# A seven-product stage on one Trainium2 core: the sixth product's weights move to another ring of buffers, and two ordinary steps stand between two pairs

## The chip, the cores and the metric

The kernel runs on one core of a Trainium2 chip. Its engines are TensorE (PE in the rows, its weight loads PEld), VectorE (DVE), ScalarE (ACT), GpSimd (POOL) and SyncE (SP, which here only issues transfers). The metric is the device time of one execution in microseconds (us); lower is better.

## The reference

Two layers of a sequence model over 256 positions of width 2048 are computed in float32, and a final norm. The change lies in the second one (the "odd" layer), whose input projection is cut here to what matters:

```
h = rms_norm(x, norm)                    # 256 x 2048
z = h @ w_in                             # 2048 x 6160, split into:
q, k, v, a_lr, gc, u, vd, gd = split(z)  # 512, 512, 1024, 16, 1024, 1024, 1024, 1024 columns
o  = gla_chunked(q, k, v, log_sigmoid(a_lr @ w_alpha + b_alpha) / 16)
yc = rms_norm(o, head_norm) * silu(gc)
yd = spatial_gating(gelu(u), gelu(vd), w_s, b_s, v_norm) * silu(gd)
x  = x + concat(yc, yd) @ w_out
```

## The kernel before, in words

**Weights.** A product with weights is done in 512 KB pieces of 128x1024. SP issues the load of a piece into a buffer of one of three rings: `raw` (3 buffers), `rx` (4) and `ry` (4). `parts` then splits the piece: ScalarE writes a rounded high half (`whi`, L138), VectorE subtracts it for the low half (`wlo`, L73), and TensorE takes three matmuls for each 512 columns and 128 rows of tokens: high weights, low weights, high weights again with the low half of the tokens. There are 4 buffers each of `whi` and `wlo`. A buffer of a ring may be loaded again once ScalarE and VectorE have read it. Outside the pairs the pieces take the rings in turn.

**Ordinary steps.** An ordinary step is one piece with both halves of the tokens, 12 matmuls (lines L146 to L148). The columns gc and gd are done this way, 32 steps in a `Stream`; while the pairs run, their pieces go through `raw` alone.

**Pairs.** The columns q and k, the two halves of vd, and the two halves of u are done as three pairs, each by `pair`. A pair takes two blocks of 512 columns as a two by two block product in seven products instead of eight. A product is four steps, a step is one piece with one form of the tokens, 6 matmuls (lines L251 to L253). In code order the products are: 

- `m12` with four pieces `x0`, loaded ahead. Behind each step GpSimd adds another 512 KB of weights onto the same buffer in flight (an accumulating transfer, L245 in the profile).
- `m3` with four pieces `y0`, and again an addition onto each of them.
- a first product into `m56` with the changed `x0`, and a second addition onto each.
- `m7` with the changed `y0`.
- a second product into the same `m56` with `x0`, now changed twice. Below this is "the last product before the tail".
- the tail: a further product into `m12` with four new pieces `z0`, and `m4` with `x0`, onto which VectorE has added `z0` (L299). The two are interleaved piece by piece, and four VectorE operations on the finished sums (L279 to L283) stand ahead of `m4`.

So a pair has 28 steps, 12 additions in flight, and 24 pieces of transfer. `weave` puts ordinary steps between its steps: 10, 8 and 10 in the three pairs; the last 4 of the 32 follow behind the third. Behind a pair its sums are used: by five or six scaled products on VectorE behind the first (`eb`, `enb`, `ebl`), by Gelu, means and variances and a normalisation (`bn_stats`, `bn_aggr`, and twelve operations in `normed`) behind the second, by Gelu behind the third. Small attention products (`gla`) run beside the second pair, and `mix` beside the end of the third. A scheduler of the framework writes each engine's queue when the program is built; each engine then works through its queue in order.

**Before the change**, `z0` is loaded into `raw`, the ring that the ordinary steps use as well. `x0` of the next pair is loaded during the tail into the ring of this pair's `y0`. So the first and third pair have `x0` in `rx` and `y0` in `ry`, the second pair the other way round.

## Time and profile before

| | |
|---|---|
| median of 3 runs | 898.17 us (897.04 to 899.81) |
| the profiled execution | 898.22 us, its span 896.5 us |
| TensorE | busy 867.7 us of the span, 97%; granted clock 0.987 of full |
| VectorE | busy 610.3 us, 68% |
| ScalarE | busy 525.9 us, 59% |
| transfers | 175.5 MB; SP's queue takes 50.6% of the 16 DMA engines' span, GpSimd's 12.1% |

Busy time is counted from an instruction's start to its end; matmuls overlap, so the distance between two starts is the better measure of TensorE's pace. The times in the rows are microseconds from the start of the span. The first pair's last product before its tail ends near 583 us, the second's near 673 us, the third's near 752 us.

### The profile page before, as it was taken

The page shows a single profiled execution, that of the slowest core. Times are in us where ns is not written, and L with a number is a line of the kernel's source. Part 1 is how long each engine was busy: PE and PEld are TensorE (multiplying, and loading weights), DVE is VectorE, ACT ScalarE, POOL GpSimd, SP SyncE. Part 2 cuts the span into 40 slices and gives each one's busy share as a digit, 9 for nine tenths or more (in the row PEclk, how much of TensorE's full clock was granted, in tenths as well). Part 3 has the DMA queues.
Part 4 walks back from the last instruction along what each step waited for, and adds up shares of the span by engine and source line. Part 5 has one row for each costly group of instructions (what it writes and reads, how often), then busy time and mean ns, then how long its engine had stood idle before and what let it go on. Part 6 is the DMA issues. An engine that isn't in the chain of part 4 may idle for free.

```text
span 896.5 us, 11877 instructions
## 1 busy us (share of the span) xinstructions
PE 867.7 (97%) x4408; PEld 724.3 (81%) x4408; DVE 610.3 (68%) x867; ACT 525.9 (59%) x764; POOL 42.4 (5%) x60
## 2 busy tenths in 40 slices
PE   9999999999999999999999999989997998899996
PEld 7888888888888888888888988866675776688886
DVE  7686556586586577665555987688566885795652
ACT  6755546766756856554445766645574764564532
POOL 0100000000000000000000002101200120000000
PEclk9999999999999999999999999999998999899998
DMA  9896555455364365665535579949953997575502
GB/s 341 337 359 208 196 178 166 151 199 166 130 213 160 110 217 179 194 206 189 186 105 188 192 217 212 293 151 243 217 165 108 254 242 254 194 231 189 187 9 94
DMA packets 50266, 175.53 MB, mean 196 GB/s; under 512 B 5648, under 2 KB 6160, under 8 KB 49952
## 3 DMA queue, kind: packets, MB, share of 16 engines
q1 hardware_dynamic: 43920, 152.65, 50.6%
q0 software_dynamic: 6144, 22.06, 12.1%
q8 instruction: 34, 0.56, 0.3%
q14 instruction: 24, 0.20, 0.1%
q10 hardware_dynamic: 144, 0.07, 0.0%
HBM read 172.66 MB, written 2.10 MB: 195 GB/s over the span
## 4 chain that ended last, share of the span: by engine, by line
PE 82%; DMA 8%; DVE 4%; issue 2%; ACT 2%; POOL 0%; ACTq 0%; POOLq 0%; DVEq 0%; SPq 0%
PE pc L315 20%; PE ps L146 13%; PE ps L148 13%; PE ps L147 13%; PE pc L314 10%; DMA raw<-in_w_in 6%; DVE wlo L73 2%; PE ps L251 2%; PE ps L252 2%; PE ps L253 2%; ACT whi L138 2%; DMA rx<-in_w_in 1%; DVE rx L299 1%; PE pc L317 1%; PE sc L500 1%
## 5 line engine op out<-in xcount | busy, mean ns | idle before, releaser
L315 PE MATMUL pc<-act,whi 128*128 128x512 f32 x768 | 269.7, 395 | 0.0
L314 PE MATMUL pc<-act,wlo 128*128 128x256 f32 x720 | 208.7, 290 | 0.0
L73 DVE TENSOR_TENSOR wlo<-rx,whi 128x1024 fp32r<-128x1024 f32 (+2 forms) x118 | 141.6, 1202 | 77.0 <-ACT whi L138 76.1
L138 ACT CAST whi<-rx 128x1024 fp32r<-128x1024 f32 (+1 forms) x115 | 119.8, 1043 | 90.0 <-PE ps L148 40.3
L73 DVE TENSOR_TENSOR wlo<-ry,whi 128x1024 fp32r<-128x1024 f32 (+2 forms) x110 | 131.7, 1199 | 58.7 <-ACT whi L138 57.5
L315 PEld LDWEIGHTS pc<-act,whi 128*128 128x128 f32 x768 | 142.8, 188 | 29.3
L73 DVE TENSOR_TENSOR wlo<-raw,whi 128x1024 fp32r<-128x1024 f32 (+2 forms) x100 | 119.1, 1191 | 67.8 <-ACT whi L138 67.4
L138 ACT CAST whi<-raw 128x1024 fp32r<-128x1024 f32 (+1 forms) x97 | 100.6, 1038 | 103.8 <-PE ps L148 46.6
L138 ACT CAST whi<-ry 128x1024 fp32r<-128x1024 f32 (+1 forms) x108 | 112.1, 1040 | 77.6 <-PE ps L148 36.6
L146 PE MATMUL ps<-whi,act 128*128 128x512 f32 (+2 forms) x352 | 133.5, 384 | 7.3 <-ACT whi L138 6.9
L314 PEld LDWEIGHTS pc<-act,wlo 128*128 128x128 f32 x720 | 135.9, 189 | 2.4 <-DVE wlo L73 0.8
L147 PE MATMUL ps<-wlo,act 128*128 128x512 f32 (+2 forms) x352 | 133.7, 380 | 0.8 <-DVE wlo L73 0.8
L148 PE MATMUL ps<-whi,act 128*128 128x512 f32 (+2 forms) x352 | 133.3, 379 | 0.0
L146 PE MATMUL ps<-whi,yt 128*128 128x512 f32 (+1 forms) x256 | 97.4, 380 | 0.0
L148 PE MATMUL ps<-whi,yt 128*128 128x512 f32 (+1 forms) x256 | 96.5, 377 | 0.0
L147 PE MATMUL ps<-wlo,yt 128*128 128x512 f32 (+1 forms) x256 | 96.3, 376 | 0.0
L146 PEld LDWEIGHTS ps<-whi,act 128*128 128x128 f32 x352 | 67.1, 192 | 22.2 <-ACT whi L138 8.8
L147 PEld LDWEIGHTS ps<-wlo,act 128*128 128x128 f32 x352 | 67.7, 192 | 14.0 <-DVE wlo L73 2.3
L148 PEld LDWEIGHTS ps<-whi,act 128*128 128x128 f32 x352 | 67.7, 192 | 11.9 <-issue 0.3
L148 PEld LDWEIGHTS ps<-whi,yt 128*128 128x128 f32 x256 | 48.2, 188 | 8.8
L147 PEld LDWEIGHTS ps<-wlo,yt 128*128 128x128 f32 x256 | 48.3, 189 | 8.4
L146 PEld LDWEIGHTS ps<-whi,yt 128*128 128x128 f32 x256 | 48.2, 188 | 8.4
(289 smaller groups left out, 1046.2 us busy)
## 6 DMA issues: line engine op xcount, KB each, us to landing
raw<-in_w_in SPq DMA_DIRECT2D x77, 512.0 KB, 4.8
ry<-in_w_in SPq DMA_DIRECT2D x64, 512.0 KB, 4.9
rx<-in_w_in SPq DMA_DIRECT2D x63, 512.0 KB, 4.6
rx<-in_w_out SPq DMA_DIRECT2D x24, 512.0 KB, 4.6
ry<-in_w_out SPq DMA_DIRECT2D x23, 512.0 KB, 4.6
rx<-in_w_in POOLq DMA_DIRECT2D x20, 512.0 KB, 9.6
raw<-in_w_out SPq DMA_DIRECT2D x17, 512.0 KB, 4.6
ry<-in_w_in POOLq DMA_DIRECT2D x16, 512.0 KB, 9.1
```

The lines of the kernel that those rows point to most:

```text
L73: nc.vector.tensor_tensor(out=o, in0=a, in1=hi.bitcast(F32), op=ALU.subtract)
L138: nc.scalar.copy(hi, raw)
L146: nc.tensor.matmul(ps[b], xh, wh, start=first, stop=False)
L147: nc.tensor.matmul(ps[b], xh, wl, start=False, stop=False)
L148: nc.tensor.matmul(ps[b], xl, wh, start=False, stop=last)
L251: nc.tensor.matmul(ps, xh, wh, start=(first and j == 0), stop=False, skip_group_check=not first)
L252: nc.tensor.matmul(ps, xh, wl, start=False, stop=False, skip_group_check=not first)
L253: nc.tensor.matmul(ps, xl, wh, start=False, stop=(j == 7), skip_group_check=not first)
L299: tc.keep_in_program_order(nc.vector.tensor_tensor(out=x0[i - 1], in0=z0[i - 1], in1=x0[i - 1], op=ALU.add))
L314: nc.tensor.matmul(ps[c][:, 1, :], wl, act[:, k, 0:T], start=False, stop=False)
L315: nc.tensor.matmul(ps[c], wh, act[:, k, :], start=(k == 0), stop=(k == KT - 1))
L317: nc.tensor.matmul(ps[c][:, 1, :], wl, act[:, k, 0:T], start=False, stop=False)
```

## The change

`z0` is loaded into the ring of `y0` (now always `ry`), and this is written earlier in the code, beside the steps of the last product before the tail. The next pair's `x0` is loaded into the ring of this pair's own `x0` (now always `rx`), written behind the `m4` step that uses the buffer last, where it was written behind the `m12` step before. The first and third pair get 8 ordinary steps instead of 10, and two ordinary steps stand behind the first and behind the second pair. Matmuls, splits, additions and transfers are the same in number.

```diff
--- before.py
+++ after.py
@@ -227,7 +227,7 @@
                 stream.step()
                 done += 1
 
-    def pair(w, ua, ub, act, forms, x0, tag, after=None):
+    def pair(w, ua, ub, act, forms, x0, after=None, own="rx", tag="ry"):
 
 
 
@@ -274,7 +274,12 @@
         s5 = mid_tile([P, 512], "s5")
         nc.scalar.copy(s5, m56)
         yield from run(m7, f7, y0, True)
-        yield from run(m56, f6, x0, False)
+
+        z0 = []
+        for i, raw in enumerate(x0):
+            z0.append(fetch(w, ua + 2, i, tag))
+            step(m56, f6, i, raw, False)
+            yield
         t = mid_tile([P, 512], "t")
         nc.vector.tensor_tensor(out=t, in0=m56, in1=s1, op=ALU.subtract)
         c22 = s1
@@ -283,16 +288,14 @@
         nc.vector.tensor_tensor(out=s5, in0=s5, in1=c22, op=ALU.subtract)
         m4 = bank()
         onward = []
-        z0 = []
         for i in range(6):
             if i < 4:
-                z0.append(fetch(w, ua + 2, i, "raw"))
                 step(m12, (act, 8, 0), i, z0[i], False)
                 yield
-                if after is not None:
-                    onward.append(fetch(w, after, i, tag))
             if i > 1:
                 step(m4, (act, 8, 1), i - 2, x0[i - 2], True)
+                if after is not None:
+                    onward.append(fetch(w, after, i - 2, own))
                 yield
             if 0 < i < 5:
 
@@ -802,7 +805,7 @@
                      between(42, keep_gd(1))])
     paired[0] = True
     x0 = [fetch(w_in1, 6, i, "rx") for i in range(4)]
-    ps, ps_k, x0 = weave(pair(w_in1, 6, 10, act2, forms2, x0, "ry", 14), stream, 10)
+    ps, ps_k, x0 = weave(pair(w_in1, 6, 10, act2, forms2, x0, 14), stream, 8)
     drain()
     eb, enb, ebl = decays
     for b in range(2):
@@ -813,6 +816,8 @@
             nc.vector.scalar_tensor_tensor(out=t[:, b, :], in0=ps_k[b], scalar=rs1[:, b:b + 1], in1=t[:, b, :],
                                            op0=ALU.mult, op1=ALU.mult)
     qt, kt, kd = eb, enb, ebl
+    for _ in range(2):
+        stream.step()
 
     nc.vector.memset(kd[64:P, 1, :], 0.0)
     osb = []
@@ -888,7 +893,7 @@
 
     vf = []
     mv = tiny.tile([P, 8, 2], F32, name="mv", tag="mv", bufs=1)
-    *vd, x0 = weave(pair(w_in1, 14, 18, act2, forms2, x0, "rx", 30), stream, 8)
+    *vd, x0 = weave(pair(w_in1, 14, 18, act2, forms2, x0, 30), stream, 8)
     for c, ps in enumerate(vd):
         t = big_tile([P, 2, 512], f"vf{c}")
         for b in range(2):
@@ -898,6 +903,8 @@
                 nc.vector.bn_stats(bs, t[:, b, i * T:(i + 1) * T])
                 nc.vector.bn_aggr(mv[:, c * 4 + b * 2 + i, :], bs)
         vf.append(t)
+    for _ in range(2):
+        stream.step()
     drain()
     ro = gla_ro[0]
     rv = rsqrt_of(mv[:, :, 1], 8, 1.0, "rv")
@@ -956,7 +963,7 @@
                                                op0=ALU.add, op1=ALU.mult)
             yield 2
 
-    *ud, _ = weave(pair(w_in1, 30, 34, act2, forms2, x0, "ry"), stream, 10)
+    *ud, _ = weave(pair(w_in1, 30, 34, act2, forms2, x0), stream, 8)
     paired[0] = False
     for c, ps in enumerate(ud):
         t = big_tile([P, 2, 512], f"yd{c}")
```

Three places in the queues, as the scheduler writes them.

**SP's queue at the end of the first pair, before.** `ry_5443`, `ry_5457`, `ry_5492` and `ry_5517` are the next pair's `x0`. `raw_5431`, `raw_5445`, `raw_5460` and `raw_5505` are `z0`, and the pieces on L132 belong to ordinary steps. `rx_5584` and `rx_5631` are the next pair's `y0`.

```order
L214 DMA ry_5443<-in_w_in1 128x1024
L214 DMA ry_5457<-in_w_in1 128x1024
L214 DMA ry_5492<-in_w_in1 128x1024
L214 DMA raw_5431<-in_w_in1 128x1024
L214 DMA ry_5517<-in_w_in1 128x1024
L214 DMA raw_5445<-in_w_in1 128x1024
L214 DMA raw_5460<-in_w_in1 128x1024
L132 DMA raw_5474<-in_w_in1 128x1024
L214 DMA raw_5505<-in_w_in1 128x1024
L214 DMA rx_5584<-in_w_in1 128x1024
L132 DMA raw_5529<-in_w_in1 128x1024
L214 DMA rx_5631<-in_w_in1 128x1024
```

**The same place after the change.** Here `ry_5327`, `ry_5339`, `ry_5369` and `ry_5381` are `z0`, `rx_5458` and `rx_5503` are the first two pieces of the next pair's `x0`, `ry_5584` and `ry_5631` of its `y0`.

```order
L214 DMA ry_5327<-in_w_in1 128x1024
L214 DMA ry_5339<-in_w_in1 128x1024
L214 DMA ry_5369<-in_w_in1 128x1024
L132 DMA raw_5471<-in_w_in1 128x1024
L214 DMA ry_5381<-in_w_in1 128x1024
L132 DMA raw_5540<-in_w_in1 128x1024
L132 DMA raw_5558<-in_w_in1 128x1024
L214 DMA ry_5584<-in_w_in1 128x1024
L214 DMA rx_5458<-in_w_in1 128x1024
L214 DMA ry_5631<-in_w_in1 128x1024
L132 DMA raw_5597<-in_w_in1 128x1024
L214 DMA rx_5503<-in_w_in1 128x1024
```

All four loads of `z0` now stand ahead of the loads for the next pair, with one ordinary piece among them, and the next pair's `x0` and `y0` alternate, each behind the last reader of the buffer that it takes.

**VectorE's queue in the tail of the first pair, before.** `rx_5039`, `rx_5041` and so on are `x0`; L299 adds `z0` onto it, `wlo<-raw` and `wlo<-rx` are splits, the L813 rows are the scaled products with the pair's sums.

```order
L73 TENSOR_TENSOR wlo_5495<-rx_5039,whi_5494 128x1024
L299 TENSOR_TENSOR rx_5041<-raw_5445,rx_5041 128x1024
L813 SCALAR_TENSOR_TENSOR enb_4714<-t_5425,rs1_4488,enb_4714 128x512
L813 SCALAR_TENSOR_TENSOR ebl_4715<-t_5425,rs1_4488,ebl_4715 128x512
L813 SCALAR_TENSOR_TENSOR enb_4714<-s1_5141,rs1_4488,enb_4714 128x512
L813 SCALAR_TENSOR_TENSOR ebl_4715<-s1_5141,rs1_4488,ebl_4715 128x512
L73 TENSOR_TENSOR wlo_5508<-raw_5505,whi_5507 128x1024
L73 TENSOR_TENSOR wlo_5520<-rx_5041,whi_5519 128x1024
L817 MEMSET ebl_4715 64x512
L73 TENSOR_TENSOR wlo_5532<-raw_5529,whi_5531 128x1024
L299 TENSOR_TENSOR rx_5043<-raw_5460,rx_5043 128x1024
L809 SCALAR_TENSOR_TENSOR eb_4713<-ps_5047,rs1q_4492,eb_4713 128x512
```

**The same place after the change.** L302 is the addition, L812 and L816 the scaled products.

```order
L73 TENSOR_TENSOR wlo_5494<-rx_5041,whi_5493 128x1024
L302 TENSOR_TENSOR rx_5043<-ry_5369,rx_5043 128x1024
L812 SCALAR_TENSOR_TENSOR eb_4713<-ps_5047,rs1q_4492,eb_4713 128x512
L816 SCALAR_TENSOR_TENSOR enb_4714<-t_5393,rs1_4488,enb_4714 128x512
L816 SCALAR_TENSOR_TENSOR ebl_4715<-t_5393,rs1_4488,ebl_4715 128x512
L816 SCALAR_TENSOR_TENSOR enb_4714<-s1_5141,rs1_4488,enb_4714 128x512
L816 SCALAR_TENSOR_TENSOR ebl_4715<-s1_5141,rs1_4488,ebl_4715 128x512
L73 TENSOR_TENSOR wlo_5507<-rx_5043,whi_5506 128x1024
L302 TENSOR_TENSOR rx_5045<-ry_5381,rx_5045 128x1024
L822 MEMSET ebl_4715 64x512
L73 TENSOR_TENSOR wlo_5520<-rx_5045,whi_5519 128x1024
L73 TENSOR_TENSOR wlo_5543<-raw_5540,whi_5542 128x1024
```

Five scaled products in a row now stand between the addition onto `rx_5043` and its split; before, four of them stood between the addition onto `rx_5041` and its split, with a piece of `z0` (`raw_5505`), and one ordinary piece (`raw_5529`) a little behind.

**VectorE's queue at the start of the third pair, before.** `ry_6247` and `ry_6288` are the third pair's first two pieces of `y0`; L936 and L938 are `normed`.

```order
L73 TENSOR_TENSOR wlo_6348<-ry_6247,whi_6347 128x1024
L899 BN_AGGR mv_5579<-bs_6226 128x2
L73 TENSOR_TENSOR wlo_6359<-ry_6288,whi_6358 128x1024
L329 TENSOR_SCALAR rv_6229<-mv_5579 128x8
L73 TENSOR_TENSOR wlo_6372<-raw_6369,whi_6371 128x1024
L331 RECIPROCAL rv_6229<-rv_6229 128x8
L936 TENSOR_SCALAR vf0_6199<-vf0_6199,mv_5579,rv_6229 128x256 x2
L936 TENSOR_SCALAR vf1_6214<-vf1_6214,mv_5579,rv_6229 128x256
L938 TENSOR_TENSOR vf0_6199<-vf0_6199,vn_5577 128x512
L936 TENSOR_SCALAR vf1_6214<-vf1_6214,mv_5579,rv_6229 128x256
L936 TENSOR_SCALAR vf0_6199<-vf0_6199,mv_5579,rv_6229 128x256
L938 TENSOR_TENSOR vf1_6214<-vf1_6214,vn_5577 128x512
```

**The same place after the change.** `ry_6283` is the first piece of `y0`, L943 and L945 are `normed`.

```order
L334 RECIPROCAL rv_6265<-rv_6265 128x8
L943 TENSOR_SCALAR vf0_6199<-vf0_6199,mv_5579,rv_6265 128x256 x2
L943 TENSOR_SCALAR vf1_6214<-vf1_6214,mv_5579,rv_6265 128x256
L945 TENSOR_TENSOR vf0_6199<-vf0_6199,vn_5577 128x512
L943 TENSOR_SCALAR vf1_6214<-vf1_6214,mv_5579,rv_6265 128x256
L943 TENSOR_SCALAR vf0_6199<-vf0_6199,mv_5579,rv_6265 128x256
L945 TENSOR_TENSOR vf1_6214<-vf1_6214,vn_5577 128x512
L943 TENSOR_SCALAR vf0_6199<-vf0_6199,mv_5579,rv_6265 128x256
L943 TENSOR_SCALAR vf1_6214<-vf1_6214,mv_5579,rv_6265 128x256
L945 TENSOR_TENSOR vf0_6199<-vf0_6199,vn_5577 128x512
L943 TENSOR_SCALAR vf1_6214<-vf1_6214,mv_5579,rv_6265 128x256
L73 TENSOR_TENSOR wlo_6384<-ry_6283,whi_6383 128x1024
```

The splits of two pieces of `y0` stood ahead of `normed` before; now all four stand behind its first eleven operations.

## Rows read from the trace of the kernel before

**Rows 1.** Engine busy time by windows, around the three tails (mean granted clock, DMA share).

```profile
588.00:612.00 24.00, 19.67 (x72) 13.56 (x71) 20.26 (x23) 12.10 (x15) 0.13 (x1) 0.93 0.60 193
673.00:703.00 30.00, 23.05 (x80) 16.36 (x79) 20.74 (x23) 14.36 (x16) 0.63 (x1) 0.89 0.49 158
718.00:724.00 6.00, 5.01 (x21) 3.34 (x19) 6.00 (x10) 2.10 (x2) 1.73 (x2) 1.00 1.07 253
748.00:785.00 37.00, 30.26 (x109) 21.32 (x108) 25.05 (x28) 18.38 (x20) 0.00 (x0) 0.91 0.60 209
```

**Rows 2.** The same view, stretches of the additions in the first and third pair.

```profile
530.00:582.00 52.00, 52.00 (x235) 43.18 (x234) 34.26 (x30) 31.94 (x35) 10.35 (x12) 1.00 0.99 248
702.00:750.00 48.00, 46.54 (x203) 37.39 (x201) 37.51 (x52) 30.54 (x33) 11.41 (x14) 1.00 1.03 260
```

**Rows 3.** Timeline of TensorE in the first tail.

```profile
589.14 0.39 PE L252 MATMUL ps<-wlo,act 128*128 128x512 f32 x1
...
590.05 0.39 PE L253 MATMUL ps<-whi,act 128*128 128x512 f32 x1
592.17 0.73 PE L146 MATMUL ps<-whi,act 128*128 128x512 f32 x2 [1.73 <-ACT whi L138]
...
593.88 0.63 PE L148 MATMUL ps<-whi,act 128*128 128x512 f32 x1
594.30 0.63 PE L147 MATMUL ps<-wlo,act 128*128 128x512 f32 x1
```

**Rows 4.** Waits of ScalarE, 748 to 784 us: total, times, longest.

```profile
ACT whi L138 <- DMA raw<-in_w_in: 15.2, 5, 5.8
```

**Rows 5.** Timeline of VectorE: prices of the operations in the tails.

```profile
588.33 0.68 DVE L279 TENSOR_TENSOR t<-ps,s 128x512 f32<-128x512 f32 x1
...
593.30 1.22 DVE L73 TENSOR_TENSOR wlo<-rx,whi 128x1024 fp32r<-128x1024 f32 x1
594.43 1.22 DVE L299 TENSOR_TENSOR rx<-raw,rx 128x1024 f32<-128x1024 f32 x1
595.57 0.74 DVE L813 SCALAR_TENSOR_TENSOR enb<-t,rs,enb 128x512 f32<-128x512 f32 x1
596.23 0.74 DVE L813 SCALAR_TENSOR_TENSOR ebl<-t,rs,ebl 128x512 f32<-128x512 f32 x1
...
705.89 0.74 DVE L898 BATCH_NORM_STATS2 bs<-vf 128x6 f32<-128x256 f32 x2
706.55 0.17 DVE L899 BATCH_NORM_AGGREGATE mv<-bs 128x2 f32<-128x6 f32 x1
...
715.15 0.20 DVE L331 RECIPROCAL rv<-rv 128x8 f32<-128x8 f32 x1 [1.07 <-ACT rv L330]
715.38 1.18 DVE L936 TENSOR_SCALAR vf<-vf,mv,rv 128x256 f32<-128x256 f32 x3
...
719.91 1.22 DVE L73 TENSOR_TENSOR wlo<-ry,whi 128x1024 fp32r<-128x1024 f32 x1
```

**Rows 6.** Timelines at the end of the first pair's last product before its tail.

```profile
578.63 1.05 ACT L138 CAST whi<-rx 128x1024 fp32r<-128x1024 f32 x1 [2.06 <-DMA rx<-in_w_in]
...
579.71 1.23 DVE L73 TENSOR_TENSOR wlo<-rx,whi 128x1024 fp32r<-128x1024 f32 x1 [1.88 <-ACT whi L138]
...
582.35 0.39 PE L252 MATMUL ps<-wlo,sums 128*128 128x512 f32 x1
```

**Rows 7.** Timeline of TensorE at the same point of the third pair.

```profile
749.14 0.39 PE L253 MATMUL ps<-whi,sums 128*128 128x512 f32 x1
...
751.60 0.51 PE L252 MATMUL ps<-wlo,sums 128*128 128x512 f32 x1 [0.76 <-DVE wlo L73]
```

**Rows 8.** Additions in flight (L245), all 36, issue to landing.

```profile
DMA to landing us min/median/max: 6.9/9.4/11.7
```

**Rows 9.** SP's loads of L214 (`fetch`) issued between 588 and 612 us.

```profile
DMA to landing us min/median/max: 3.6/4.6/5.0
```

**Rows 10.** All 36 of SP's loads of L214, the whole span.

```profile
DMA to landing us min/median/max: 3.5/4.9/15.4
```

## The prediction

> **What bounds the kernel now.** I looked first at the table of busy time above: TensorE is busy 97% of the span, so a gain can only come from the few places where it is not, or where it runs at half pace. The view by windows shows them: around the three tails TensorE is idle and the granted clock falls under 1.00, and at 718 us there is a smaller gap [rows 1]. In the stretch between, with the additions, it is busy all 52 us of 52 in the first pair [rows 2].
>
> What these windows lose I count by pace, not by idle time. In the timeline two matmuls four places apart start 0.91 us apart, so one takes 0.2275 us at full clock; behind an idle time of 1.73 us they start 0.42 us apart, the lower of the two levels [rows 3]. The four windows hold 72, 80, 21 and 109 matmuls [rows 1], worth 16.4, 18.2, 4.8 and 24.8 us. (Some of them are smaller, so the loss is if anything a little higher.) The windows last 24, 30, 6 and 37 us. **The loss is 7.6 + 11.8 + 1.2 + 12.2 = 32.8 us**; nothing the change does at these places can give more.
>
> Which wait ends last there: ScalarE waits for a load into `raw`, 15.2 us in five waits in the third tail [rows 4]. That is `z0` together with the ordinary pieces: some seven pieces go through three buffers, a buffer with `z0` is held until VectorE has added it onto `x0`, and SP works through its queue in order. VectorE is not idle meanwhile: it is busy 20.3 of 24 us in the first tail and 6.0 of 6 at 718 us [rows 1]. So behind the wait for the load stands a second limit, and the question is how much of the 32.8 us it keeps.
>
> **What the change removes.** `z0` no longer shares `raw`. Its four loads stand ahead of all others of the tail in SP's queue, behind the last readers of `y0`. In the first pair that is where the next `x0` was loaded before, into the same buffers of `ry`; so `z0` takes those loads' place and is there before the tail. I cost the wait for `raw` at nothing left.
>
> **What stays: VectorE's queue in the tails.** I add up what it must do, in the order of the changed queue, from the end of the last product before the tail (the first operation on the finished sums waits for it) to the split that TensorE needs, and set TensorE's matmuls up to there against it. Prices [rows 5]: an operation on the sums 0.68; a split or an addition 1.135 (from start to start, 593.30 to 595.57 for two); a scaled product 0.66; two variances 0.66, an aggregate 0.08 to 0.17, together 1.0 for eight; the first eleven operations of `normed` 719.91 - 715.38 = 4.5. The cast on ScalarE ahead of a split takes 1.05 [rows 6].
>
> - First tail, to the split of `x0`'s last piece: 4 on the sums 2.7, 4 additions and 7 splits 12.5, 5 scaled products 3.3, a small fill taken as one more, 0.7; and 0.5 because the last piece's cast has only that fill beside it: 19.7 us. TensorE has 69 matmuls up to there, 15.7, and four small transposes, estimated at 0.5: 16.2. **It waits 3.5 us.**
> - Second tail and on to the third pair's first piece of `y0`, which now stands behind `normed`: 4 on the sums 2.7, 4 additions and 18 splits 25.0, the closing sum 0.7, variances 2.6 and 1.0, `normed` 4.5, its wait for the square root 1.07 and the reciprocal 0.2 [rows 5], the last cast 1.1: 38.9 us. TensorE has 145 matmuls, 33.0. **It waits 5.9 us.** This takes the place of the 11.8 and the 1.2. The two ordinary steps behind each pair are counted in (24 matmuls against 2 splits, 5.5 us against 2.3): without them the wait would be 3.2 us longer.
> - Third tail: 4 on the sums 2.7, 4 additions and 7 splits 12.5, five short operations of `mix` at half a scaled product or a little more, 2.3: 17.5, against 69 matmuls and four small ones, 16.3. **1.2 us.**
>
> Below, these waits could be about half as long, if the buffers of `whi` and `wlo` (4 each) let VectorE start further ahead than I take; above they stand as they are.
>
> **What moves: the additions in flight.** The first and third pair have two ordinary steps less, so TensorE comes to the end of the last product sooner, by one step, 12 x 0.2275 = 2.7 us (the second is taken behind that point). In the first pair the last addition landed just in time: ScalarE waited 2.06 us for it, the split ended at 580.94, TensorE needed it at 582.35, so 1.4 us were left [rows 6]. Against 2.7 - 1.4 = 1.3 us stands that one ordinary piece and two of `z0` less are loaded beside the additions, while the DMA engines' share there is 0.99 [rows 2]. Bounds 0 and 1.3; I take 0, since three loads out of some two dozen transfers in 52 us are worth more than 1.3 us. In the third pair two matmuls took 2.46 us instead of 0.45 there, 2.0 us lost [rows 7]. One step less of cover makes it 4.7 at most. But four pieces of later steps, which SP had fetched early into the idle `ry`, and two of `z0` no longer run beside the additions, `z0`'s four do: 0 at least. I take the row's **2.0 us**.
>
> The Trainium skill ("DMA: Bandwidth & Descriptors", section "Queues, rings and completion order") says that each DMA engine goes in turn between the queues that have work, packet by packet. By it fewer loads from SP let the additions land sooner, the 2.0 us would go and the sum would be 877.7; the trace agrees insofar as landing spreads from 6.9 to 11.7 us with the company [rows 8].
>
> **What else moves.** The next pair's `x0` is fetched later, behind its buffer's last split in `m4`. The last of four is issued at 19.7 us in the first tail's count. Its own split stands 8.2 us further down VectorE's queue (six splits 6.8, a sum 0.7, a scaled product 0.7), and its cast takes 1.05, so it may take 7.1 us to land. Loads in this stretch took 3.6 to 5.0 us [rows 9]. Cost nothing. The next `y0` is issued between, behind the additions that free its buffers, and is needed four steps later still.
>
> **The clock.** One fall cost 24 x 0.07 = 1.7 us in the first tail (0.93 granted) [rows 1]. Of the waits left, one in the first tail and one at `normed` come out near 2 us at a stretch, near the 1.73 us that stood before a fall [rows 3]. Half of a fall each: **1.7 us**.
>
> **Sum.** Left over: 3.5 + 5.9 + 1.2 + 2.0 + 1.7 = 14.3. Gained: 32.8 - 14.3 = 18.5. The profiled execution took 898.22 us (span 896.5 and 1.7 around it), the median of the runs shown is 898.17. **898.2 - 18.5 = 879.7 us.**
>
> **The rivals.**
> - *VectorE is hidden after all.* The pieces split ahead cover its queue, nothing of the 32.8 is left: 865.4 us. For it: VectorE is busy only 68% of the span by the table, and four pieces may wait ready. Against: the operations on the sums can't start before the product ends, and the counts above give it more work than TensorE at both boundaries. Chance 0.12.
> - *The additions become the bound.* Both bounds above hold, 1.3 and 4.7, and their waits bring two more falls: 879.7 + 1.3 + 2.7 + 3.4 = 887.1. For it: DMA shares of 0.99 and 1.03 [rows 2]; against: fewer loads beside them. Chance 0.17.
> - *The next `x0` comes late, and the kernel is not faster.* Place: the first steps of the second and third pair. If the loads take what the slowest took, 15.4 us [rows 10], the last piece is 8.3 us late at two boundaries, 16.6, and each such wait falls as the second tail did, 30 x 0.11 = 3.3 [rows 1], 6.6 instead of the 1.7 counted: 901.2. It decides from a landing of about 14 us. For it: the window behind 718 us has a DMA share of 1.07 [rows 1], and additions of the next pair begin while these loads run. Against: the DMA share in the tails is 0.49 to 0.60 [rows 1], and additions start only behind the first piece's split. The Trainium skill ("Trainium Kernel Development and Optimization", section "Best Practices") has the rule to overlap transfers with computing by double buffers; by it this shorter lead is a loss, and the time would be this rival's. Chance 0.05.
>
> **How the numbers follow.** My forecast has 0.66: 879.7, its own range 873 (waits halved, no fall) to 887 (the upper ends and two whole falls). With the rivals the range that leaves out no more than two in ten is 870 to 890. A difference of 0.3%, 2.7 us, is about what a measurement of this kernel can tell from no change. All cases but the last are faster by more: 0.94 (a little off for what none of them names); within 0.3% 0.02; slower 0.04.
>
> **What would show it.** Right: no wait of ScalarE for a load into `ry` or `raw` in the tails; VectorE without a pause there; TensorE's waits in the tails are for `whi` or `wlo` behind a busy VectorE, the longest ahead of the third pair's `y0`, behind `normed`. Wrong: waits for the landing of `rx` at a pair's start (the late fetch), waits of over 5 us for `rx` at the last product before a tail (the additions), or tails without any wait (hidden).

## The result, and the profile after

| | before | after |
|---|---|---|
| median | 898.99 us (4 runs) | 885.11 us (883.41 to 888.22, 4 runs) |
| ratio | 1 | 0.9852, 95% interval 0.9818 to 0.9886 |
| the profiled execution, its span | 898.22, 896.5 us | 884.4, 882.7 us |
| mean granted clock | 0.987 | 0.992 |

The kernel is 13.9 us faster; 18.5 were forecast. The time lies in the range, 5.4 us above the predicted 879.7.

The first view is again engine busy time by windows, of the changed kernel, over the stretches that answer to [rows 1, 2] (columns as there: TensorE, its weight loads, VectorE, ScalarE, GpSimd, granted clock, DMA share, GB/s).

```profile
530.00:582.00 52.00, 50.64 (x226) 41.52 (x225) 32.61 (x29) 31.05 (x35) 10.35 (x12) 1.00 0.97 239
586.00:610.00 24.00, 20.33 (x73) 14.67 (x72) 22.45 (x26) 13.06 (x14) 0.34 (x1) 0.86 0.76 240
671.00:697.00 26.00, 23.12 (x95) 17.07 (x94) 23.03 (x28) 17.61 (x20) 0.00 (x0) 1.00 0.55 183
711.00:717.00 6.00, 5.23 (x22) 3.74 (x21) 6.00 (x9) 2.78 (x3) 1.47 (x2) 1.00 1.02 227
736.00:771.00 35.00, 32.81 (x134) 25.47 (x133) 28.07 (x31) 20.19 (x21) 1.07 (x2) 0.95 0.84 275
```

Counted as in the prediction (length less 0.2275 us for each matmul), the last four rows lose 7.4, 4.4, 1.0 and 4.5 us. Before they lost 7.6, 11.8, 1.2 and 12.2. The first row holds 226 matmuls where there were 235 [rows 2], 2.0 us lost where nothing was lost before. Together the loss is 19.3 us against 32.8, a gain of 13.5; 13.9 were measured. So the second tail gave what was hoped, the third most of it, the first almost nothing, and the stretch of the additions in the first pair lost.

**The wait that was removed.** Waits of ScalarE between 745 and 785 us in the changed kernel (total, times, longest), the stretch of [rows 4]:

```profile
ACT whi L138 <- DVE rx L302: 5.3, 4, 2.4
ACT whi L138 <- PE ps L148: 3.6, 2, 3.0
ACT whi L138 <- DMA rx<-in_w_in: 2.8, 1, 2.8
```

The 15.2 us for loads into `raw` are gone. What ScalarE waits for now is VectorE's addition onto `x0` (L302), TensorE (L148), and, once, a landing in `rx`: an addition in flight.

**The first pair's end.** Timelines of ScalarE, VectorE and TensorE at the last product before the tail, the place of [rows 6]; the bracket is the idle time ahead and what ended it.

```profile
579.14 1.05 ACT L138 CAST whi<-rx 128x1024 fp32r<-128x1024 f32 x1 [2.80 <-DMA rx<-in_w_in]
580.22 1.23 DVE L73 TENSOR_TENSOR wlo<-rx,whi 128x1024 fp32r<-128x1024 f32 x1 [2.62 <-ACT whi L138]
580.24 0.49 PE L251 MATMUL ps<-whi,sums 128*128 128x512 f32 x1 [0.59 <-ACT whi L138]
581.50 0.50 PE L252 MATMUL ps<-wlo,sums 128*128 128x512 f32 x1 [0.76 <-DVE wlo L73]
...
582.53 0.40 PE L253 MATMUL ps<-whi,sums 128*128 128x512 f32 x1
...
584.77 0.68 DVE L284 TENSOR_TENSOR t<-ps,s 128x512 f32<-128x512 f32 x1
...
603.07 1.23 DVE L73 TENSOR_TENSOR wlo<-rx,whi 128x1024 fp32r<-128x1024 f32 x1 [0.52 <-ACT whi L138]
603.09 0.80 PE L251 MATMUL ps<-whi,act 128*128 128x512 f32 x1 [0.82 <-ACT whi L138]
...
605.06 0.63 PE L252 MATMUL ps<-wlo,act 128*128 128x512 f32 x1
605.49 0.63 PE L253 MATMUL ps<-whi,act 128*128 128x512 f32 x1
```

The last addition of the first pair let the cast start at 578.63 us before [rows 6]; now it starts at 579.14. TensorE comes a step earlier and waits. Behind the late split three further splits stand in VectorE's queue, so the first operation on the sums starts at 584.77, though TensorE's last matmul of the product started at 582.53. From 584.77 to the end of the last split at 604.3 VectorE takes 19.5 us (19.7 were counted). At the end of the tail TensorE waits 0.82 us once more, and eleven matmuls from 605.06 on start 0.43 us apart, the lower level of the clock.

**The third pair's end.** The same for the place of [rows 7], with the issues of GpSimd's additions in flight (L245), the first, fifth and last of twelve, ahead.

```profile
699.37 0.85 POOL L245 DMA_DIRECT2D rx<-in_w_in  x1 [50.90 <-DVE bs L903]
...
714.65 0.85 POOL L245 DMA_DIRECT2D ry<-in_w_in  x1 [6.10 <-DVE wlo L73]
...
735.12 0.85 POOL L245 DMA_DIRECT2D rx<-in_w_in  x1 [2.94 <-DVE wlo L73]
...
746.36 1.05 ACT L138 CAST whi<-rx 128x1024 fp32r<-128x1024 f32 x1 [2.78 <-DMA rx<-in_w_in]
747.46 0.50 PE L251 MATMUL ps<-whi,sums 128*128 128x512 f32 x1 [0.87 <-ACT whi L138]
748.71 0.50 PE L252 MATMUL ps<-wlo,sums 128*128 128x512 f32 x1 [0.76 <-DVE wlo L73]
...
749.81 0.63 PE L253 MATMUL ps<-whi,sums 128*128 128x512 f32 x1
```

From the first issue to the cast behind the last landing the additions take 47.0 us. Before, they took 46.9 us (702.37 to 749.24). The two waits of TensorE are hardly longer than before, where the first was 0.81 us and the second is in [rows 7], but now the clock falls behind them:

```profile
750.34 0.51 PE L251 MATMUL ps<-whi,sums 128*128 128x512 f32 x1 [0.81 <-ACT whi L138]
```

**The late fetch.** SP's loads of L214 between 584 and 612 us, issue to landing, as in [rows 9]:

```profile
DMA to landing us min/median/max: 3.9/4.8/5.8
```

TensorE waits for none of them. The four loads of L214 issued between 560 and 582 us, those of `z0`, run beside the last additions and took far longer:

```profile
DMA to landing us min/median/max: 10.0/12.7/13.5
```

### The profile page after: what moved, and what is told of

It is laid out like the page before. It is cut to its first block, busy times and chain, and to the rows that moved or that the text cites. A ratio compares the mean times of both kernels' runs of the same rounds, so it can differ in the third digit from the quotient of the medians.

```text
span 882.7 us, 11885 instructions
## 1 busy us (share of the span) xinstructions
PE 861.9 (98%) x4408; PEld 722.5 (82%) x4408; DVE 608.8 (69%) x867; ACT 525.4 (60%) x764; POOL 42.6 (5%) x60
## 4 chain that ended last, share of the span: by engine, by line
PE 83%; issue 5%; DVE 5%; DMA 4%; POOL 1%; ACT 1%; ACTq 0%; POOLq 0%; DVEq 0%
PE pc L318 20%; PE ps L146 13%; PE ps L147 13%; PE ps L148 13%; PE pc L317 10%; DMA rx<-in_w_in 3%; DVE wlo L73 3%; PE ps L251 2%; PE ps L253 2%; PE ps L252 2%; DVE rx L302 1%; PE pc L320 1%; ACT whi L138 1%; POOL rx L245 1%; PE sc L503 1%
## 5 line engine op out<-in xcount | busy, mean ns | idle before, releaser
L73 DVE TENSOR_TENSOR wlo<-rx,whi 128x1024 fp32r<-128x1024 f32 (+2 forms) x126 | 151.0, 1200 | 78.8 <-ACT whi L138 77.0
L138 ACT CAST whi<-rx 128x1024 fp32r<-128x1024 f32 (+1 forms) x123 | 128.4, 1045 | 112.5 <-PE ps L148 42.2
L73 DVE TENSOR_TENSOR wlo<-ry,whi 128x1024 fp32r<-128x1024 f32 (+2 forms) x114 | 136.3, 1198 | 64.6 <-ACT whi L138 63.6
L138 ACT CAST whi<-ry 128x1024 fp32r<-128x1024 f32 (+1 forms) x112 | 116.2, 1040 | 77.4 <-PE ps L148 43.1
L73 DVE TENSOR_TENSOR wlo<-raw,whi 128x1024 fp32r<-128x1024 f32 (+2 forms) x88 | 104.1, 1185 | 50.5 <-ACT whi L138 49.7
L146 PE MATMUL ps<-whi,act 128*128 128x512 f32 (+2 forms) x352 | 131.7, 379 | 1.5 <-ACT whi L138 0.9
L147 PE MATMUL ps<-wlo,act 128*128 128x512 f32 (+2 forms) x352 | 131.6, 374 | 0.2
L148 PE MATMUL ps<-whi,act 128*128 128x512 f32 (+2 forms) x352 | 131.1, 372 | 0.0
L138 ACT CAST whi<-raw 128x1024 fp32r<-128x1024 f32 (+1 forms) x85 | 87.9, 1036 | 68.9 <-PE ps L148 37.0
L148 PE MATMUL ps<-whi,yt 128*128 128x512 f32 (+1 forms) x256 | 96.4, 376 | 0.0
L146 PEld LDWEIGHTS ps<-whi,act 128*128 128x128 f32 x352 | 66.2, 189 | 15.6 <-ACT whi L138 2.2
L148 PEld LDWEIGHTS ps<-whi,act 128*128 128x128 f32 x352 | 66.6, 189 | 11.5
L148 PEld LDWEIGHTS ps<-whi,yt 128*128 128x128 f32 x256 | 48.2, 188 | 8.9
```

Of the source, the lines that this page charges most:

```text
L73: nc.vector.tensor_tensor(out=o, in0=a, in1=hi.bitcast(F32), op=ALU.subtract)
L138: nc.scalar.copy(hi, raw)
L146: nc.tensor.matmul(ps[b], xh, wh, start=first, stop=False)
L147: nc.tensor.matmul(ps[b], xh, wl, start=False, stop=False)
L148: nc.tensor.matmul(ps[b], xl, wh, start=False, stop=last)
```

## The experiments

**Theory.** The additions in flight of a pair take a time of their own, some 47 us, whatever the ordinary steps do. The two steps taken out of the first and third pair were TensorE's work meanwhile. Without them TensorE waits at the end of the last product, VectorE's tail starts late because of it, and the clock falls. **Rivals:** VectorE's queue alone sets the tails; the ordinary steps between the pairs are what costs; the loads of `z0` beside the additions are. The letters in an expectation hold for that expectation. Times of different groups of runs are compared by their ratios to the kernel before.

**Rings alone.** The change with 10, 8 and 10 steps in the pairs and none between.

```diff
-    ps, ps_k, x0 = weave(pair(w_in1, 6, 10, act2, forms2, x0, 14), stream, 8)
+    ps, ps_k, x0 = weave(pair(w_in1, 6, 10, act2, forms2, x0, 14), stream, 10)
...
-    for _ in range(2):
-        stream.step()
...
-    for _ in range(2):
-        stream.step()
...
-    *ud, _ = weave(pair(w_in1, 30, 34, act2, forms2, x0), stream, 8)
+    *ud, _ = weave(pair(w_in1, 30, 34, act2, forms2, x0), stream, 10)
```

> One part alone: z0 and the next x0 in their new rings, but 10, 8 and 10 ordinary steps in the pairs and none between. Theory A (VectorE's queue holds the tails, and the additions of the first and third pair land late because the pair is shorter): the waits for additions at the end of the last product before the tail go (about 2 us in the first pair and 3 to 4 with the clock in the third), but both boundaries lose the two steps that covered VectorE (3.2 us each), so about 885 to 888, near the changed kernel. Rival B (the gain comes from the two steps between the pairs, not from the rings): 893 or more. Rival C (DMA alone is the bound, VectorE costs nothing): about 879.

Measured: 874.22 us, ratio 0.9726 (0.9707 to 0.9745), less than any of the times expected. By the ratios the rings give 24.6 of 899 us, and the moved steps take some 11 of them back; the 3.2 us for each boundary that theory A took from the prediction are not lost. Windows of this kernel over the same five places:

```profile
530.00:582.00 52.00, 52.00 (x235) 43.16 (x234) 34.51 (x30) 32.44 (x35) 10.36 (x12) 1.00 0.99 249
586.00:612.00 26.00, 24.57 (x109) 18.86 (x108) 25.74 (x28) 15.30 (x18) 2.31 (x3) 1.00 0.73 227
671.00:697.00 26.00, 23.13 (x95) 17.24 (x94) 24.49 (x32) 17.58 (x19) 2.60 (x3) 1.00 0.80 243
705.00:711.00 6.00, 5.14 (x21) 3.51 (x20) 6.00 (x10) 2.48 (x3) 1.44 (x3) 1.00 1.06 251
724.00:759.00 35.00, 34.35 (x151) 27.79 (x150) 29.19 (x31) 24.05 (x26) 0.98 (x2) 1.00 0.88 291
```

The first stretch holds 235 matmuls again, the others lose 1.2, 4.4, 1.2 and 0.6 us: 7.4 in all against 19.3. The whole difference lies in the first pair (8.2) and at the end of the third (3.9); the second boundary, with or without the two steps, loses the same.

In the first tail TensorE now has an ordinary step more ahead of `x0`'s last piece. From the end of the product to that piece, here and, in the second row, in the change:

```profile
583.60:603.10 19.50, 18.67 (x84) 14.93 (x82) 19.41 (x21) 11.20 (x13) 0.00 (x0) 1.00 0.64 212
582.70:603.00 20.30, 16.87 (x71) 12.40 (x70) 19.69 (x22) 10.45 (x13) 0.00 (x0) 1.00 0.61 198
```

VectorE is busy for nearly all of either; TensorE does 84 matmuls beside it instead of 71. So the step is cover for VectorE's queue in the tail, and not for the additions alone.

**Steps alone.** The kernel before with the moved steps only.

```diff
-    ps, ps_k, x0 = weave(pair(w_in1, 6, 10, act2, forms2, x0, "ry", 14), stream, 10)
+    ps, ps_k, x0 = weave(pair(w_in1, 6, 10, act2, forms2, x0, "ry", 14), stream, 8)
...
+    for _ in range(2):
+        stream.step()
...
+    for _ in range(2):
+        stream.step()
...
-    *ud, _ = weave(pair(w_in1, 30, 34, act2, forms2, x0, "ry"), stream, 10)
+    *ud, _ = weave(pair(w_in1, 30, 34, act2, forms2, x0, "ry"), stream, 8)
```

> The other part alone: 8 ordinary steps in each pair and two behind the first and the second, but z0 in the ring of the ordinary steps and the next x0 in the ring of y0, as before. Theory A: z0 still shares three buffers, so ScalarE still waits for loads into that ring in all three tails; 894 to 899. Rival B (the steps are the gain): about 885.

Measured: 906.17 us, ratio 1.0078 (1.0062 to 1.0095): slower than before, and than either time expected. Alone, too, the moved steps cost, 7.0 us by the ratio.

**Without the loads of `z0`** (the product with `z0` takes the buffers of `y0`; four loads are left out in each pair).

```diff
-            z0.append(fetch(w, ua + 2, i, tag))
+            z0.append(y0[i])
```

> The changed kernel without the 12 loads of z0: the sixth product takes the buffers of y0 as they stand, so that part of the computation is left out. Nothing else differs in work. Theory A with the additions delayed by z0's loads beside them: the last addition onto x0 in the first pair lands 2 to 4 us sooner than the 11 us of the changed kernel, TensorE's wait there (2 us) and the late start of VectorE's tail (1.6 us) go, and the third pair's wait shrinks: about 879 to 881. Rival D (the additions have a pace of their own, whatever else is loaded): the last addition lands as late as now, 884 to 886.

Measured: 877.55 us, ratio 0.9760 (0.9732 to 0.9787). TensorE's waits at the end of the last product are gone in both pairs, those of the first tail stay (longest 1.68 us). There the first operation on the sums starts as far behind the product's last matmul as in the change, 2.2 us:

```profile
582.21 0.40 PE L253 MATMUL ps<-whi,sums 128*128 128x512 f32 x1
...
584.45 0.68 DVE L284 TENSOR_TENSOR t<-ps,s 128x512 f32<-128x512 f32 x1
```

So VectorE's tail is late without a late split too; three splits stand ahead of the sums in both. By the same count the first tail (586 to 610 us, 84 matmuls) loses 4.9 us, where the change loses 7.4: the clock does not fall here, behind the same wait. Fewer transfers beside the additions do let them land sooner; the first row is issue to landing of the additions between 525 and 585 us here, the second that of the change:

```profile
DMA to landing us min/median/max: 5.7/8.9/10.6
```

```profile
DMA to landing us min/median/max: 5.7/9.0/12.2
```

**Scaled products later.** The change, the six scaled products pinned behind the two ordinary steps (five of them stood ahead of the last splits in the tail).

```diff
+    for _ in range(2):
+        stream.step()
     for b in range(2):
-        nc.vector.scalar_tensor_tensor(out=eb[:, b, :], ...)
+        tc.keep_in_program_order(nc.vector.scalar_tensor_tensor(out=eb[:, b, :], ...))
...
-    for _ in range(2):
-        stream.step()
```

> The changed kernel with the six scaled products behind the first pair written after the two ordinary steps and kept in program order, so that in VectorE's queue they stand behind the splits of x0's last pieces. The result is the same. Theory A: TensorE's two waits in the first tail (2.0 and 1.0 us) shrink by the 3.3 us of five products, and if no idle time near 1.7 us is left, the fall of the clock behind them (2.3 us) goes too: about 880. Rival C (DMA is the bound) or a late x0 of the next pair: no change, 885.

Measured: 884.94 us, ratio 0.9842 (0.9828 to 0.9857): no gain. In the first tail the longest wait fell from 1.69 to 0.84 us and the clock did not fall. The third pair's first addition went out 2.2 us earlier (697.22), its last at 735.29, where it was 735.12. Their chain took 49.3 us here, 47.0 in the change; why is not shown. TensorE, earlier, waited for them:

```profile
739.94 0.51 PE L251 MATMUL ps<-whi,sums 128*128 128x512 f32 x1 [1.07 <-ACT whi L138]
...
747.60 0.49 PE L251 MATMUL ps<-whi,sums 128*128 128x512 f32 x1 [0.91 <-ACT whi L138]
```

By the same count the first tail loses 4.9 us instead of 7.4, and the stretch from 736 to 771 us, with 123 matmuls, 7.0 instead of 4.5. What VectorE saves is given back at the additions.

**Ten in the first pair only** (none between the first and second; the rest as in the change).

```diff
-    ps, ps_k, x0 = weave(pair(w_in1, 6, 10, act2, forms2, x0, 14), stream, 8)
+    ps, ps_k, x0 = weave(pair(w_in1, 6, 10, act2, forms2, x0, 14), stream, 10)
...
-    for _ in range(2):
-        stream.step()
```

> The change, but the first pair keeps its 10 ordinary steps and none stands between the first and the second pair; the third pair keeps 8, and two stand between the second and the third. Theory A (the two steps taken out of a pair were the cover of its additions in flight; without it TensorE waits at the end of the last product, VectorE's tail starts late, and the clock falls): in the change's trace the first pair lost about 2 us there, 1.6 us by the late start and 2.3 us in a clock fall, so 885 - 6 = about 879 us, with the third pair's waits as in the change. Rival B (the first pair has slack; what costs is the steps at 8 in the third pair with the tail's VectorE queue): about 884 us, no more than 1 us from the change.

Measured: 880.17 us, ratio 0.9787 (0.9774 to 0.9801). The first pair's waits at the end of the product are gone, the third pair's stand. The gain on the change is 5 to 6 us, less than the 8.2 us lost in the first pair: the third pair's additions now take 49.0 us from the first issue (694.16) to the cast behind the last landing, and TensorE, there sooner, waits four times:

```profile
736.63 0.49 PE L251 MATMUL ps<-whi,sums 128*128 128x512 f32 x1 [1.16 <-ACT whi L138]
737.89 0.50 PE L252 MATMUL ps<-wlo,sums 128*128 128x512 f32 x1 [0.77 <-DVE wlo L73]
...
743.16 1.04 ACT L138 CAST whi<-rx 128x1024 fp32r<-128x1024 f32 x1 [2.82 <-DMA rx<-in_w_in]
744.26 0.50 PE L251 MATMUL ps<-whi,sums 128*128 128x512 f32 x1 [0.86 <-ACT whi L138]
745.52 0.50 PE L252 MATMUL ps<-wlo,sums 128*128 128x512 f32 x1 [0.76 <-DVE wlo L73]
```

So part of what one pair gains is given back at the next pair's additions.

**Eight in all pairs, none between.** The change without its two pairs of steps between; eight steps follow behind the third pair.

```diff
-    for _ in range(2):
-        stream.step()
...
-    for _ in range(2):
-        stream.step()
```

> 8 ordinary steps in each of the three pairs and none between pairs; the 8 steps left all follow behind the third pair. This keeps the exposed additions of the change and takes away the two places between the pairs. Theory A (the missing cover costs, the place between the pairs is harmless or a small help): no faster than the change, 885 to 891 us; by the prediction's count the two steps between pairs are worth 3.2 us at each boundary with a loaded VectorE. Rival B (the steps between the pairs are themselves what costs, since their pieces are split ahead of the next pair's): faster than the change by several us, 875 to 880 us.

Measured: 888.86 us, ratio 0.9877 (0.9858 to 0.9897). Taking the steps between away gives nothing back: what costs is that they are missing in the pairs. In the third pair the fifth addition goes out 10.7 us after the first (15.3 in the change), the twelve take 43.9 us to the last landing, and TensorE waits once at the last product, 0.76 us, with no fall behind it; but by the same count the stretch from 730 to 765 us, with 130 matmuls, still loses 5.4 us. TensorE at the end of the first pair's product:

```profile
581.87 0.49 PE L251 MATMUL ps<-whi,sums 128*128 128x512 f32 x1 [0.83 <-ACT whi L138]
583.12 0.50 PE L252 MATMUL ps<-wlo,sums 128*128 128x512 f32 x1 [0.77 <-DVE wlo L73]
```

**Without the second additions** (the four second additions onto `x0` are left out in the first and in the third pair).

```diff
-        yield from run(m56, f5, x0, True, ub + 2)
+        yield from run(m56, f5, x0, True, None if ub != 18 else ub + 2)
```

> The change, but the four second additions onto x0 are left out in the first and in the third pair (eight of 36 transfers; the products that use x0 then lack one term). Theory A: the waits at the end of the last product in both pairs (2.0 and 2.8 us) and the clock falls beside them (2.3 and 1.5 us) go, and VectorE's first tail starts on time; 876 to 879 us, and the tails keep their VectorE waits. Rival C (VectorE's queue alone sets the tails, and an earlier end of the last product only makes TensorE wait longer for VectorE there): 883 to 885 us.

Measured: 876.68 us, ratio 0.9749 (0.9733 to 0.9765), as the theory had it; the first tail keeps its waits (longest 1.69 us). With eight steps in the pairs, the stretch of the additions is full again:

```profile
530.00:582.00 52.00, 52.00 (x235) 43.16 (x234) 35.81 (x31) 33.42 (x36) 6.92 (x8) 1.00 0.79 198
```

**Two steps between, with ten in the pairs.** The rings alone, and two of the last four steps taken to between the first and second pair (the first of the two), or the second and third.

```diff
+    for _ in range(2):
+        stream.step()
```

> The rings alone (10, 8 and 10 steps in the pairs), and two ordinary steps between the first and the second pair, taken from the four that follow behind the third pair. It gives the change's place between pairs without taking cover from a pair. By the prediction's count two such steps are worth up to 3.2 us where TensorE waits for VectorE; the rings alone lose about 2.5 us in the first tail, so 871.5 to 873 us against 874.2. Rival (the place is worth nothing: the pieces of the two steps only push the next pair's splits further down VectorE's queue): 874 to 876 us.

> The rings alone, and two ordinary steps between the second and the third pair, taken from the four behind the third pair. The rings alone lose 5 to 6 us from the second tail to the third pair's y0; by the prediction's count two steps there are worth 3.2 us: about 871 us against 874.2. Rival (the place is worth nothing): 874 to 876 us.

Measured: 874.21 us, ratio 0.9739 (0.9719 to 0.9759), and 877.25 us, ratio 0.9762 (0.9746 to 0.9778). The place is worth nothing at the first boundary, and at the second the time is worse than with the rings alone. There GpSimd's first, fifth and last issue of the third pair, and TensorE at the last product, were:

```profile
692.52 0.85 POOL L245 DMA_DIRECT2D rx<-in_w_in  x1 [50.90 <-DVE bs L901]
...
707.88 0.85 POOL L245 DMA_DIRECT2D ry<-in_w_in  x1 [5.42 <-DVE wlo L73]
...
730.13 0.85 POOL L245 DMA_DIRECT2D rx<-in_w_in  x1 [2.62 <-issue]
...
742.49 0.49 PE L251 MATMUL ps<-whi,sums 128*128 128x512 f32 x1 [0.97 <-ACT whi L138]
```

The fifth addition, the first onto `y0`, goes out 15.4 us after the first; 5.4 us GpSimd waits for the split that stands behind `normed` in VectorE's queue. In the rings alone it is 11.8 us.

**Eleven instead of ten.** The rings alone with 11 steps in the first and third pair.

```diff
-    ps, ps_k, x0 = weave(pair(w_in1, 6, 10, act2, forms2, x0, 14), stream, 10)
+    ps, ps_k, x0 = weave(pair(w_in1, 6, 10, act2, forms2, x0, 14), stream, 11)
...
-    *ud, _ = weave(pair(w_in1, 30, 34, act2, forms2, x0), stream, 10)
+    *ud, _ = weave(pair(w_in1, 30, 34, act2, forms2, x0), stream, 11)
```

> The rings alone with 11 ordinary steps instead of 10 in the first and in the third pair, two left behind the third pair. If cover of the additions still decides at 10 steps, a further step in each takes away the last waits at the end of the third pair's last product (0.6 us) and lets the tails start earlier: 872 to 873.5 us. If ten steps cover them: 874 us, no change; if the steps behind the third pair were cover there: 875 to 877 us.

Measured: 875.26 us, ratio 0.9744 (0.9728 to 0.9759), not to be told from the rings alone: an eleventh step gives nothing more.

**`normed` spread.** The rings alone, `normed` pinned in program order and spread over the third pair.

```diff
     def normed(c):
+        yield 20 + 2 * c
...
-                nc.vector.tensor_scalar(out=t, ...)
+                tc.keep_in_program_order(nc.vector.tensor_scalar(out=t, ...))
+                yield 3
-            nc.vector.tensor_mul(...)
+            tc.keep_in_program_order(nc.vector.tensor_mul(...))
```

> The rings alone, with 10, 8 and 10 steps in the pairs and none between, and the twelve operations of normed kept in program order and spread over the third pair's first twenty steps, so that the splits of y0 no longer stand behind eleven of them. If it is the place of normed in VectorE's queue that costs (the prediction's 5.9 us held 4.5 of it): the wait ahead of y0, 0.8 us in the rings alone, goes and some of the short ones before it, 872 to 873 us against 874.2. If it is the amount of VectorE's work up to there, not its place: 874 us, the waits move to the pieces behind.

Measured: 878.27 us, ratio 0.9770 (0.9756 to 0.9783): neither, but slower than the rings alone. The wait ahead of `y0` went, as expected; TensorE came to the additions sooner, and waited there (and the clock fell behind these waits):

```profile
736.82 0.50 PE L251 MATMUL ps<-whi,sums 128*128 128x512 f32 x1 [0.81 <-ACT whi L138]
738.08 0.50 PE L252 MATMUL ps<-wlo,sums 128*128 128x512 f32 x1 [0.76 <-DVE wlo L73]
```

**Steps between the second and third pair, `normed` behind `y0`.** The kernel of 877.25 us with `normed` pinned as above, from `yield 34 + 2 * c` on.

> The rings alone with two ordinary steps between the second and the third pair (877.25 us, 3.0 us over the rings alone), and now the twelve operations of normed pinned behind all four splits of the third pair's y0. Theory A (the additions in flight of the third pair set its end: with the two steps between, y0's splits and so its first addition, the fifth of the pair, stand behind normed and go out 15.4 us after the first, 11.8 in the rings alone; that time is missing at the end of the last product, where TensorE waits 1.0 and 0.8 us and the clock falls): the fifth addition goes out 8 to 12 us after the first, the last lands about 45 us after the first's issue instead of 48.8, the two waits and the fall go: 872 to 874 us. Rival (the two steps themselves cost, by their loads beside the additions or by their place): 876 to 878 us, with the additions as long as before.

Measured: 875.30 us, ratio 0.9752 (0.9733 to 0.9771), between the two expectations. The trace is plain, the time is not: first, fifth and last issue, and the last cast behind a landing:

```profile
692.73 0.86 POOL L245 DMA_DIRECT2D rx<-in_w_in  x1 [50.90 <-DVE bs L901]
...
704.96 0.85 POOL L245 DMA_DIRECT2D ry<-in_w_in  x1 [2.30 <-issue]
...
726.14 0.85 POOL L245 DMA_DIRECT2D rx<-in_w_in  x1 [1.98 <-DVE wlo L73]
...
737.33 1.05 ACT L138 CAST whi<-rx 128x1024 fp32r<-128x1024 f32 x1 [2.73 <-DMA rx<-in_w_in]
```

The fifth addition is out 12.2 us after the first, the last lands 4 us sooner, and TensorE's waits at the last product are gone. But the intervals of the two ratios overlap, so how much of the 3 us this place costs is not settled. No version was faster than the rings alone; the one with two steps at the first boundary took the same time.

## Why the prediction was right, and where its terms were off

- **The bound, and what the change removes: right.** The waits for `raw` are gone, 24.6 us by the rings alone, of the 32.8 counted as the most.
- **VectorE's queue: right in length, its start too early.** The first tail's count was 19.7 us, 19.5 were measured; but it began at the product's end, and VectorE began some 2 us later (see the first tail below). Second tail and `y0`: 5.9 forecast and half a fall, 5.4 measured. The longest single wait was not ahead of the third pair's `y0`, where it was expected (0.7 us), but in the first tail (1.7).
- **The additions in the first pair: the step that failed.** I took 0 between the bounds 0 and 1.3, "since three loads out of some two dozen transfers in 52 us are worth more than 1.3 us". They were worth nothing: the cast behind the last addition starts 0.5 us later than before. The runs without `z0` and without second additions show that transfers matter to the additions' end; but SP issued five loads between 560 and 572 us in the change as before, `z0`'s in place of the next `x0`'s, 10.0 to 13.5 us in flight. The stretch lost 2.0 us, about the bound of 1.3 and these 0.5: TensorE would have needed the last split at 579.7 us and had it at 581.5.
- **The first tail: under-sized.** 7.4 us lost, 3.5 and half a fall (0.85) forecast. Three splits that the count left out stand ahead of the first operation on the sums, so VectorE starts it 2.2 us behind the start of the product's last matmul. Without a fall the tail loses 4.9 us (no loads of `z0`). At its end there is a whole fall of 2.2 us (11 matmuls by 0.2) where I had half a one. That the tail has an ordinary step less than with ten in the pair was in the count of 69 matmuls; what that step is worth was not seen: with it the tail loses 1.2 us.
- **The third pair: the waits right, a fall not counted.** 2.0 and 1.2 forecast, 4.5 measured. The two waits at the last product lose 2.2 us (746.20 to 749.05 us for three matmuls), the fall behind them about 1.5, the rest is the tail.
- **The two steps between the pairs: wrong.** "Without them the wait would be 3.2 us longer" does not hold. With ten steps in the pairs they gave nothing at the first boundary and cost 3.2 us, by the ratios, at the second. The waits they should cover (0.84 and 0.45 us with two steps at the first boundary) stand at the last pieces of `m4`, ahead of them in TensorE's queue.
- **Sum.** 2.0 + 3.0 + (5.4 - 6.75) + 1.3 = 5.0 us more than forecast; the gain was 4.6 less. The time lay in the range, but nearer to the rival's 887.1 than to 879.7; that three terms were too small and one too large, and that the range held both cases, is part of why the forecast stands.
- **The rivals.** *VectorE hidden*: no, 5.4 us stay at the second boundary, and 5.6 in the rings alone. *The additions become the bound*: in the first pair yes (2.0 lost, 1.3 in the rival), and falls came with it; in the third pair the waits lost 2.2, not 4.7. So its 887.1, 2 us too high, came near through other terms than its own. *Late `x0`*: no; loads took at most 5.8 us. The Trainium skill's rule to overlap by double buffers ("Trainium Kernel Development and Optimization", section "Best Practices") would have made the shorter lead a loss; this trace shows none.
- **The rule on the queues.** The additions' landing falls from at most 12.2 to 10.6 us when `z0`'s loads are left out. The Trainium skill ("DMA: Bandwidth & Descriptors", section "Queues, rings and completion order") has each DMA engine take turns between the queues that have work; with that the trace agrees. My use of it, 877.7 us, did not hold, since as many loads were issued beside the last additions as before.

What the runs show, by ratios: the first pair's two steps are worth 5 to 6 us where they stand (the change against ten in the first pair only; the place between gives nothing). The two steps between the second and third pair cost 3.2 us (877.25 us against the rings alone). Eight steps instead of ten in the third pair cost some 2.2 more (880.17 against 877.25 us), though there the intervals overlap by a hair. How the first pair's loss divides, 2.0 us at the additions and the rest in VectorE's tail and the fall, is read from the traces. The theory's fixed time of the additions did not hold: they took 44 to 50 us. In the third pair, with all transfers, it goes with the first addition onto `y0`: 43.9 to 44.6 us where that is out 10.7 to 12.2 us after the first (three versions), 47.0 to 49.3 us where it is out 15.1 to 15.4 us after (five versions). What sets the 2 us within the latter stays open.

## What to carry to other kernels

Work that stands between a transfer and its use is cover, even where no wait shows, and the same work can cover another engine's queue: before taking steps out of a stage, measure how long its chain of transfers takes from first issue to last landing, and how long the other engine's queue is, and compare both with the work left. And test the two halves of a change apart: here one half was worth 24.6 us and the other cost some 11.

## What the runs showed of the hardware that was not expected

Twelve additions in flight of 512 KB took 44 to 50 us from first issue to last landing in the first and third pair of every version with all its transfers.

The granted clock fell behind pairs of waits none of which was as long as the 1.73 us of [rows 3]: 0.87 and 0.76 us in the change, 0.81 and 0.76 with `normed` spread. With eight in all pairs, 0.83 and 0.77 us were followed by matmuls at full pace; so was, without the loads of `z0`, a wait of 1.68 us in the first tail, where the change's 1.69 and 0.82 were followed by a fall. What decides is not settled here.
